# A hybrid decoder layer: the last pair's values in two halves, and the output projection's tiles moved into later steps

## The chip, the cores and the metric

The kernel runs on one core of one Trainium2 chip. The metric is the device time of one execution in microseconds (us). TensorE is called PE below, VectorE DVE, ScalarE ACT, GpSimd POOL; SP issues the transfers.

## The reference

One decoder layer on a sequence of 1024 tokens of width 1024, in float32. The part that matters here is the mixer: eight attention heads of width 64 beside four recurrent heads of width 128, whose outputs are joined and projected.

```python
h = rmsnorm(x, mix_pre_norm[layer])
proj = h @ w_in[layer]
q_a, k_a, v_a, q_h, f_h, i_h, g_h = jnp.split(proj, splits, axis=-1)
attn = dilated_mixture_attention(q_a.reshape(ahead), k_a.reshape(ahead), v_a.reshape(ahead), slopes)
attn = rmsnorm(attn.reshape(B, S, ATTN_WIDTH), attn_out_norm[layer])
rec = hgrn2_recurrence(q_h, f_h, i_h, g_h, lower_bounds[layer], hgrn_out_norm[layer])
mixed = jnp.concatenate([attn, rec], axis=-1) @ w_out[layer]
x = x + rmsnorm(mixed, mix_post_norm[layer])
h = rmsnorm(x, mlp_pre_norm[layer])
ff = jnp.square(jax.nn.relu(h @ w_ff1[layer])) @ w_ff2[layer]
x = x + rmsnorm(ff, mlp_post_norm[layer])
```

## The kernel before

Every float32 product is made of three matmuls in a rounded format: each operand is split into a high part (a copy on ACT, line 83) and a low part (a subtraction on DVE, line 84), and `three_pass` multiplies high by high, high by low and low by high (lines 87 to 89). So each weight tile of 128x1024 costs a transfer (`w_load`), an ACT copy and a DVE subtraction (`w_split`, called through `w_get`), before PE can use it. Two raw tiles are in the chip at a time: a tile's transfer is issued when the tile two places ahead of it in the list has been split.

The recurrent heads come first, then the attention in 64 steps: step s is head s // 8 and block of 128 queries s % 8 (the block number is called b). Heads are taken in pairs (0,1), (2,3), (4,5), (6,7), and a pair shares its projections. A step does in this order: the exponentials of step s+1 (ACT), the scores of step s+2 (`look`: matmuls into one or two banks of tag `s`, read by DVE), the transposes of its own block (`turn`: up to two PSUM banks of tag `t`, emptied by ACT into `pth` and by DVE into `ptl`), the weighted sum of the values (`weigh`, tile `pov`) every other step, the turning back of that sum (`finish`), the step's hook, and then filler. Scores with up to four blocks of keys take one bank, later ones two. At the change of pairs, step 46 for the last pair, the scores of s+2 come only after the transposes, since the next pair's keys must be there.

Filler is PE work from a queue of generators. Each yields an estimated cost of 650 for three matmuls of 128x512, called a unit here, and `fill` takes units until the allowance of the step is used up. `drain` takes all that is left. In heads 0 to 5 the filler is the projection of the next pair (`attn_proj`): its queries (`aq`), values (`av`) and keys (`ak`), each in two halves of 512 tokens with eight units a half. The value halves are turned by four transposes (`v_turn`, tile `pvt`, into a bank of tag `mm`, emptied by ACT and DVE, lines 617 and 618). The second half of the keys is evacuated later (`keys_off`, tile `kf`, through `put_off`), copied into place by ACT, POOL and transfers.

In heads 6 and 7 the filler is `early_out`: the recurrent half of the output projection for the first four row blocks. For a row block t it needs the turned row (`row_turn(t, 0)`: four transposes, tile `pmt`, a bank of tag `t`, split into `emt`) and the first four weight tiles of the output, list places WO0 to WO0+3 (`raw28` to `raw31`). It fills two banks of tag `mm` (`pwe`) at once. The banks of each tag are two, taken in turn. Each engine works through its instructions in the order of the program text; there is no scheduler behind it.

The order around the change is written by hand in `hooks`, by step: before, the output tiles are split in steps 44, 45, 47 and 48, and rows turned in steps 45, 46, 48 and 49. `WO_TAG` says in which buffers the split tiles lie: none means the rotating weight buffers `wh` and `wl`.

Of the kernel before, what the change touches and what calls it, by code (L numbers as in the profile page):

```python
# [18 lines left out]
T = 1024  # L19
# [16 lines left out]
def hymba_layer(ctx, tc, x, w_in, w_out, w_ff1, w_ff2, g_pre, lb_logits, g_mix, g_post,  # L36
# [21 lines left out]
    def half(name, dtype=F32):  # L58
        return sp.tile([P, 512], dtype, tag="half", name=name, bufs=2)
# [63 lines left out]
    def w_get(i, ahead=1):  # L123
        while done[1] < min(i + 1 + ahead, len(stream)):
            w_split()
        return parts[i]
# [24 lines left out]
    for i in range(4 * HH, 4 * HH + 3 * (AH // 2)):  # L151
        stream.append((w_in[i], None))
    WO0 = len(stream)
    WO_TAG = (None, None, ("S", "S"), ("S", "BT"), ("S", "S"), ("S", "T"), ("T", "T"), ("T", "T"))

    def wo_dest(k, tags):
        return lambda: (slab(tags[0], f"woh{k}", F32R), slab(tags[1], f"wol{k}", F32R))
# [25 lines left out]
    def drain():  # L183
        while queue:
            n = len(queue)
            fill(1e9)
            assert len(queue) < n or not queue
# [380 lines left out]
    first_done = [False] * (AH // 2)  # L568
    A0 = 4 * HH

    put_off = []

    def keys_off(pr, stacks, pm, hf):

# [11 lines left out]
    def attn_proj(pr):  # L586
        stacks = [{}, {}]
        box = [None]
        w = w_get(A0 + 3 * pr, 0)
        for i in range(2):  # L590
            stacks[i]["q"] = slab("S", f"q{pr}_{i}", F32R)
        for hf in range(2):
            sl = slice(hf * 512, hf * 512 + 512)
            for n, cost in enumerate(proj_t(w, f"aq{pr}", hf, box)):
                if hf == 0 and n == 4:
                    w_get(A0 + 3 * pr)
                yield cost
            full = half(f"qf{pr}{hf}")
            V.scalar_tensor_tensor(full, box[0], 0.125, rrow[:, sl], op0=ALU.mult, op1=ALU.mult)
            lo = half(f"ql{pr}{hf}", F32R)  # L600
            for i, (a, b) in enumerate(halves):
                S.activation(stacks[i]["q"][a:b, sl], full[a:b], AF.Copy)
                G.tensor_tensor(out=lo[a:b], in0=full[a:b], in1=f32(stacks[i]["q"][a:b, sl]), op=ALU.subtract)
            nc.sync.dma_start(out=f32(stacks[0]["q"][64:128, sl]), in_=f32(lo[0:64]))
            nc.sync.dma_start(out=f32(stacks[1]["q"][0:64, sl]), in_=f32(lo[64:128]))
            yield 650.0
        w = w_get(A0 + 3 * pr + 1, 0)
        vs = slab("V8", f"v{pr}", F32R, (P, NT, 2, 2, 64))
        late = None

        def v_turn(full, hf):
            pt = bank("mm", f"pvt{pr}{hf}")
            for j in range(4):
                TE.transpose(pt[:, j * P:(j + 1) * P], full[:, j * P:(j + 1) * P], ident)
            ptv = pt.rearrange("p (j h d) -> p j h d", j=4, h=2)
            dst = vs[:, hf * 4:hf * 4 + 4]
            S.activation(dst[:, :, :, 0, :], ptv, AF.Copy)
            V.tensor_tensor(out=dst[:, :, :, 1, :], in0=ptv, in1=f32(dst[:, :, :, 0, :]), op=ALU.subtract)
        for hf in range(2):
            sl = slice(hf * 512, hf * 512 + 512)  # L620
            n = 0
            for cost in proj_t(w, f"av{pr}", hf, box):
                n += 1
                if n == 4 and late is not None:
                    v_turn(*late)
                    cost += 450.0
                if n == 5 and hf == 0:
                    w_get(A0 + 3 * pr + 1)
                yield cost
            full = half(f"vf{pr}{hf}")  # L630
            V.tensor_tensor(out=full, in0=box[0], in1=rrow[:, sl], op=ALU.mult)
            late = (full, hf)
            yield 650.0
        while pr > 0 and not first_done[pr - 1]:
            yield None
        w = w_get(A0 + 3 * pr + 2, 0)
        for i in range(2):
            stacks[i]["kh"] = slab("S", f"kh{pr}_{i}", F32R)
            stacks[i]["kl"] = slab("S", f"kl{pr}_{i}", F32R)
        for hf in range(2):  # L640
            sl = slice(hf * 512, hf * 512 + 512)
            n = 0
            for cost in proj_t(w, f"ak{pr}", hf, box):
                n += 1
                if n == 3 and hf == 0:
                    v_turn(*late)
                    cost += 450.0
                if n == 6 and hf == 0:
                    w_get(A0 + 3 * pr + 2)
                yield cost  # L650
            if hf == 0 and pr == AH // 2 - 1:
                early_rows()
            if hf == 0:
                keys_off(pr, stacks, box[0], hf)
            else:
                put_off.append((pr, stacks, box[0], hf))
            pairs[pr] = (stacks, vs)
            yield 650.0
# [6 lines left out]
    def load_bias(hd):  # L665
        if hd < AH and hd not in bts:
            bts[hd] = slab("BT", f"bt{hd}") if hd < AH - 1 else early["table"][:, 0]
            nc.sync.dma_start(out=bts[hd], in_=bias_tab[hd])
# [89 lines left out]
    def load_gain(name, tag, src):  # L758
        gains[name] = slab(tag, name)
        nc.sync.dma_start(out=gains[name], in_=src.partition_broadcast(P))  # L760
# [16 lines left out]
    def early_sums():  # L777
        early["sum"] = [wide.tile([P, 2, D], F32, tag="A", name=f"esum{q}") for q in range(NE // 2)]
# [12 lines left out]
    def row_rec(t):  # L791
        gain = gains["early"] if t < NE else gains["gmix"][:, :AW]
        G.tensor_tensor(out=rec_row(t), in0=rec_row(t), in1=gain, op=ALU.mult)
# [27 lines left out]
    def row_turn(t, which, late=False):  # L821

        if t < NE and which == 0:
            dst = early["mt"][t // 2][:, t % 2]
        else:
            if (t, 1) not in mts and (t, 0) not in mts or t < NE:
                mts[t] = slab("V8", f"mt{t}", F32R, (P, 2, 2, 4, P))
            dst = mts[t][:, which]
        mts[t, which] = dst
        src = rec_row(t) if which == 0 else rows[t][:, AW:]  # L830
        pt = bank("pv" if late else "t", f"pmt{t}_{which}")
        for j in range(4):
            TE.transpose(pt[:, j * P:(j + 1) * P], src[:, j * P:(j + 1) * P], ident)
        split_into(dst[:, 0], dst[:, 1], pt.rearrange("p (j c) -> p j c", j=4))
# [12 lines left out]
    def early_out(t):  # L847
        pms = [bank("mm", f"pwe{t}_{hf}") for hf in range(2)]
        for j in range(4):
            while j >= done[1] - WO0:  # L850
                yield None
            for hf, pm in enumerate(pms):
                sl = slice(hf * 512, hf * 512 + 512)
                three_pass(pm, [mts[t, 0][:, i, j] for i in range(2)], [w[:, sl] for w in parts[WO0 + j]], j == 0, j == 3)
                if j == 3:
                    S.activation(early_sum(t)[:, sl], pm, AF.Copy)
                yield 650.0
# [103 lines left out]
    for h in range(HH):  # L961
# [8 lines left out]

    hooks = {
        43: lambda: [row_rec(0), row_rec(1)],
        44: lambda: [row_rec(2), row_rec(3), w_get(WO0, 0)],
        45: lambda: [drain(), w_get(WO0 + 1, 0), row_turn(0, 0)],
        46: lambda: [early_sums(), row_turn(1, 0), queue.extend(early_out(t) for t in range(NE))],
        47: lambda: [w_get(WO0 + 2, 0), load_bias(AH - 1)],
        48: lambda: [load_gain("gmix", "R", g_mix), w_get(WO0 + 3, 0), row_turn(2, 0)],
        49: lambda: row_turn(3, 0),
        55: lambda: [row_load(t) for t in range(3)],
        59: lambda: [row_norm(0), row_gain(0)],  # L980
        60: lambda: [row_norm(1), row_gain(1)],
# [6 lines left out]
    for s in range(n_steps):  # L988
        if s % 16 == 6:
            first_done[s // 16] = True  # L990
        hd, b = steps[s]
        ready, to_weigh = to_weigh, []
        raise_(s + 1)
        fresh = (s + 2) % 16 == 0
        if not fresh:
            look(s + 2)
        turn(hd, b, exped.pop(s))
        if b % 2:
            to_weigh.append((hd, b // 2))
        to_fold, last_fold = [(i, g, weigh(i, g)) for i, g in ready], to_fold  # L1000
        if fresh and s + 2 < n_steps:
            while pairs[(s + 2) // 16] is None:
                fill(1.0)
            if (s + 2) // 16 + 1 < AH // 2:
                drain()
                queue.append(attn_proj((s + 2) // 16 + 1))
            look(s + 2)
        for i, g, a in last_fold:
            finish(i, g, *a)
        hooks.get(s, lambda: None)()  # L1010
        if b in (7, 0, 1) or s == 46:
            while put_off:
                keys_off(*put_off.pop())
        fill(3240.0 - 340.0 * b if s < n_steps - 20 else 1000.0 if s < n_steps - 16 else 1175.0)
    for i, g, a in to_fold:
        finish(i, g, *a)
    to_fold = [(i, g, weigh(i, g)) for i, g in to_weigh]
# [804 lines left out]
```

## Time and profile before

| | us |
|---|---|
| median of 3 runs | 1268.75 |
| lowest and highest | 1268.53, 1270.63 |
| the profiled execution | 1270.28 |
| its span, first to last instruction | 1268.5 |
| PE busy | 1237.2 |
| DVE busy | 883.2 |
| ACT busy | 532.7 |
| POOL busy | 293.3 |

The mean granted clock of PE over the span is 0.997. The profile gives the busy time of each engine, what ended each idle time of an engine, and a timeline of instructions with their starts. A matmul's row is longer than its share of PE's time, because matmuls are pipelined: the distance between two starts tells what one costs. Rows of DVE and ACT overlap their neighbours by a little for the same reason. The attention steps lie between 310 and 554 us, and step 46 is near 490 us.

### The profile page before, as it was taken

To read this page: it belongs to the slowest core of one execution; us is meant where nothing else is said; L and a number is where in the kernel's file an instruction comes from. 1 tells how busy PE (TensorE), PEld (TensorE's weight loads), DVE (VectorE), ACT (ScalarE), POOL (GpSimd) and SP (SyncE) were. 2 spreads that over 40 slices of the span, in tenths; PEclk is the share of its full clock that TensorE was granted. 3 is DMA by queue.
4 is the path that set the end of the run, shared out by engine and by line. 5 is a ranking of instruction groups with operands and counts; after the bars stand their busy time and mean duration, and the time that the engine had idled before them with its cause. 6 is when DMAs were issued, how large, how long until landed. Compare 5 with 4: busy or idle time off the path is not lost. (4 is left out here: it accounts for less than half of the span.)

```text
span 1268.5 us, 17269 instructions
## 1 busy us (share of the span) xinstructions
PE 1237.2 (98%) x6512; PEld 1056.1 (83%) x6512; DVE 883.2 (70%) x1530; ACT 532.7 (42%) x970; POOL 293.3 (23%) x304
## 2 busy tenths in 40 slices
PE   8999999999999998999999999999999999999997
PEld 8898989888888887877778888888878888888886
DVE  5686868675666666667659766666675777698956
ACT  7523232223565555664565412222236544344412
POOL 0000000012121214044350387557531000000012
PEclk9999999999999999999999999999999999999999
DMA  5201111123232323244342545345368464434413
GB/s 208 68 18 50 34 51 34 34 83 84 68 87 64 88 63 115 96 143 155 100 158 83 207 166 183 126 149 183 125 250 338 155 210 133 156 94 132 168 62 135
DMA packets 58578, 153.98 MB, mean 121 GB/s; under 512 B 4992, under 2 KB 12928, under 8 KB 58240
## 3 DMA queue, kind: packets, MB, share of 16 engines
q1 hardware_dynamic: 58496, 152.89, 35.7%
q8 instruction: 51, 0.84, 0.3%
q14 instruction: 31, 0.25, 0.1%
HBM read 106.73 MB, written 39.85 MB: 116 GB/s over the span
## 5 line engine op out<-in xcount | busy, mean ns | idle before, releaser
L87 PE MATMUL f<-bh,ah 128*128 128x512 f32 x392 | 152.5, 389 | 0.0
L88 PE MATMUL f<-bl,ah 128*128 128x512 f32 x392 | 152.5, 389 | 0.0
L89 PE MATMUL f<-bh,al 128*128 128x512 f32 x392 | 152.5, 389 | 0.0
L84 DVE TENSOR_TENSOR al<-ar,ah 128x1024 fp32r<-128x1024 f32 x49 | 60.6, 1238 | 48.0 <-ACT ah L83 17.6
L88 PEld LDWEIGHTS f<-bl,ah 128*128 128x128 f32 x392 | 73.6, 188 | 15.4
L87 PEld LDWEIGHTS f<-bh,ah 128*128 128x128 f32 x392 | 73.6, 188 | 15.3
L89 PEld LDWEIGHTS f<-bh,al 128*128 128x128 f32 x392 | 73.6, 188 | 15.2
L83 ACT ACTIVATE ah<-ar 128x1024 fp32r<-128x1024 f32 x49 | 52.1, 1064 | 50.1 <-DMA ar<-actd 21.3
L719 DVE TENSOR_TENSOR ptl<-pt,pth 128x512 fp32r<-128x512 f32 (+2 forms) x96 | 50.4, 552 | 23.4 <-ACT pth L718 23.3
L1737 POOL TENSOR_SCALAR fp<-fss 128x1 f32<-128x1 f32 x8 | 3.4, 428 | 266.4 <-ACT fd L1734 266.4
L718 ACT ACTIVATE pth<-pt 128x512 fp32r<-128x512 f32 (+2 forms) x96 | 43.4, 486 | 42.5 <-PE pt L715 41.0
L691 DVE CUSTOM_DVE_ANT_0 p<-ps,bt 128x512 f32<-128x512 f32 (+2 forms) x84 | 44.4, 553 | 19.9 <-PE ps L689 19.7
L1250 POOL TENSOR_TENSOR e<-x,e 128x512 f32<-128x512 f32 x14 | 20.6, 1475 | 136.1 <-DVE x L1201 136.1
L702 ACT ACTIVATE p<-p,nm 128x128 f32<-128x128 f32 (+3 forms) x64 | 49.4, 772 | 2.6 <-DVE nm L695 2.1
L79 POOL TENSOR_SCALAR ms<-hss 128x8 f32<-128x8 f32 x4 | 0.8, 198 | 209.1 <-DVE hss L552 209.1
L715 PE MATMUL pt<-ident,p 128*128 128x128 f32 x288 | 43.0, 276 | 5.4 <-DVE emt L84 3.0
L83 ACT ACTIVATE bh<-br 128x1024 fp32r<-128x1024 f32 x28 | 29.8, 1063 | 43.4 <-PE f L89 38.0
L748 POOL TENSOR_TENSOR anat<-anat,rd 128x128 f32<-128x128 f32 x32 | 14.6, 456 | 129.5 <-DVE anat L747 122.6
L715 PEld LDWEIGHTS pt<-ident,p 128*128 128x128 f32 x288 | 33.6, 141 | 9.9 <-DVE ptl L719 4.0
L732 PE MATMUL pov<-pth,v 128*128 128x256 f32 (+1 forms) x160 | 41.4, 292 | 0.0
L1604 DVE TENSOR_TENSOR acc<-f,acc 128x512 f32<-128x512 f32 x52 | 33.8, 685 | 8.2 <-PE f L89 8.2
L732 PE MATMUL pov<-ptl,v 128*128 128x256 f32 (+1 forms) x160 | 38.6, 286 | 0.5 <-DVE ptl L719 0.5
(1616 smaller groups left out, 3877.5 us busy)
## 6 DMA issues: line engine op xcount, KB each, us to landing
ar<-actd SPq DMA_DIRECT2D x49, 512.0 KB, 3.6
raw<-in_w_in_dram SPq DMA_DIRECT2D x28, 512.0 KB, 3.6
w1r<-in_w_ff_dram SPq DMA_DIRECT2D x14, 1024.0 KB, 6.3
br<-in_w_ff_dram SPq DMA_DIRECT2D x14, 1024.0 KB, 7.8
actd<-e SPq DMA_DIRECT2D x17, 768.0 KB, 4.1
actd<-e SPq DMA_DIRECT2D x11, 1024.0 KB, 4.0
xr<-in_x_dram SPq DMA_DIRECT2D x8, 512.0 KB, 8.6
raw<-in_w_out_dram SPq DMA_DIRECT2D x8, 512.0 KB, 3.5
```

The source lines that it names most:

```text
L83: S.activation(hi, src, AF.Copy)
L84: eng.tensor_tensor(out=lo, in0=src, in1=f32(hi), op=ALU.subtract)
L87: TE.matmul(dst, lhs[0], rhs[0], start=start, stop=False)
L88: TE.matmul(dst, lhs[0], rhs[1], start=False, stop=False)
L89: TE.matmul(dst, lhs[1], rhs[0], start=False, stop=stop)
L691: V.tensor_tensor_reduce(out=pe[:, k0:k0 + n], in0=pS[:, :n], in1=bts[hd][:, o:o + n], scale=1.0, scalar=-3.0e38, op0=ALU.add, op1=ALU.max ...
L702: S.activation(pe[:, :nk], pe[:, :nk], AF.Exp, bias=nm[:, b:b + 1], accum_out=dn[:, b:b + 1])
L715: TE.transpose(pt[:, j * P:(j + 1) * P], pe[:, jj * P:(jj + 1) * P], ident)
L718: S.activation(hi, src, AF.Copy)
L719: V.tensor_tensor(out=lo, in0=src, in1=f32(hi), op=ALU.subtract)
L732: TE.matmul(po[:, c0:256], vst, pt[j // 4][q][:, j % 4, c0:], start=j == 0 and q == 0, stop=j == nj - 1 and q == 1)
L1604: V.tensor_tensor(out=acc_at(p, i), in0=pm, in1=acc_at(p, i), op=ALU.add)
```

## The change

Three things change together, all around the last pair (heads 6 and 7). The number of instructions on PE, DVE and ACT stays the same, and they are of the same shapes.

- The second half of the last pair's values (`av31`) is no longer projected before its keys, in heads 4 and 5, but by a generator of its own, `v_rest`, which is put into the queue in step 45 after the drain. Its turning (`pvt31`) stands in the hook of step 50.
- The first four output tiles are split in steps 48, 49, 50 and 51, the rows turned in steps 48, 51, 52 and 53, and `early_out` joins the queue in step 50. The buffers of the tiles change accordingly: tiles 0 and 1 take slabs, tiles 2 and 3 the rotating buffers.
- The allowance of filler is smaller in steps 30 to 43 (2560 - 270 b, before 3240 - 340 b) and larger from step 48 on (1600, before 1175). The second half of the keys is evacuated in step 47, before in step 46.

In program order PE's filler is afterwards: in step 45 five units (three of the keys, two of `av31`), in step 46 two and in step 47 one of `av31`, in step 48 the turned row 0 and the last three of `av31`, in step 49 none, in step 50 the turning of the values and three units of the output, in steps 51 to 53 a turned row each and two, three and two units, and from step 54 to step 62 two or three units. After the last transposes of step 63 there is none; before there was one.

```diff
-    WO_TAG = (None, None, ("S", "S"), ("S", "BT"), ("S", "S"), ("S", "T"), ("T", "T"), ("T", "T"))
+    WO_TAG = (("S", "S"), ("S", "BT"), None, None, ("S", "S"), ("S", "T"), ("T", "T"), ("T", "T"))
...
+        split = pr == AH // 2 - 1
+
+        def v_rest(wv):
+            sl = slice(512, T)
+            yield from proj_t(wv, f"av{pr}", 1, box)
+            full = half(f"vf{pr}1")
+            V.tensor_tensor(out=full, in0=box[0], in1=rrow[:, sl], op=ALU.mult)
+            yield 650.0
+            rest.append(lambda: v_turn(full, 1))
+        if split:
+            deferred.append(v_rest(w))
-        for hf in range(2):
+        for hf in range(1 if split else 2):
...
-                if n == 6 and hf == 0:
+                if n == 6 and hf == 0 and not split:
                     w_get(A0 + 3 * pr + 2)
...
-        44: lambda: [row_rec(2), row_rec(3), w_get(WO0, 0)],
-        45: lambda: [drain(), w_get(WO0 + 1, 0), row_turn(0, 0)],
-        46: lambda: [early_sums(), row_turn(1, 0), queue.extend(early_out(t) for t in range(NE))],
-        47: lambda: [w_get(WO0 + 2, 0), load_bias(AH - 1)],
-        48: lambda: [load_gain("gmix", "R", g_mix), w_get(WO0 + 3, 0), row_turn(2, 0)],
-        49: lambda: row_turn(3, 0),
+        44: lambda: [row_rec(2), row_rec(3)],
+        45: lambda: [drain(), queue.append(deferred.pop())],
+        46: lambda: load_bias(AH - 1),
+        48: lambda: [w_get(WO0, 0), row_turn(0, 0)],
+        49: lambda: [w_get(WO0 + 1, 0)],
+        50: lambda: [drain(), load_gain("gmix", "R", g_mix), early_sums(), w_get(WO0 + 2, 0), rest.pop()(),
+                     queue.extend(early_out(t) for t in range(NE))],
+        51: lambda: [w_get(WO0 + 3, 0), row_turn(1, 0)],
+        52: lambda: row_turn(2, 0),
+        53: lambda: row_turn(3, 0),
...
-        if b in (7, 0, 1) or s == 46:
+        if b in (7, 0, 1):
...
-        fill(3240.0 - 340.0 * b if s < n_steps - 20 else 1000.0 if s < n_steps - 16 else 1175.0)
+        if s < n_steps - 20:
+            fill(3240.0 - 340.0 * b if s < n_steps - 34 else 2560.0 - 270.0 * b)
+        else:
+            fill(1000.0 if s < n_steps - 16 else 1600.0)
```

More of the change, by code (lines that the diff above doesn't have):

```diff
@@ L569, in hymba_layer @@
     A0 = 4 * HH
-    put_off = []
+    put_off, deferred, rest = [], [], []
     def keys_off(pr, stacks, pm, hf):
```

## The prediction

> **What bounds the kernel now.** I read the busy table of the page first, then who waited for whom on the matmul engine between 310 and 640 us (the attention steps and the output projection behind them), then the stages of 10 us, then the timeline around each idle place; the waits give a total, a count and the longest.
>
> ```profile
> PE 1237.2 (98%) x6512; PEld 1056.1 (83%) x6512; DVE 883.2 (70%) x1530; ACT 532.7 (42%) x970; POOL 293.3 (23%) x304
> ```
>
> ```profile
> 490.00:500.00 10.00, 5.81 (x33) 5.09 (x32) 6.29 (x13) 4.63 (x8) 4.91 (x4) 0.83 0.20 64
> ```
>
> ```profile
> PE pt L715 <- DVE ptl L719: 2.3, 4, 0.9
> ...
> PE pov L732 <- DVE ptl L719: 0.5, 1, 0.5
> ```
>
> PE is busy for 98% of the span, and the change adds or removes no matmul. So the time can move only by what PE idles and by the clock at which it works. The stage from 490 to 500 us is the one sick stage: PE busy 5.81 of 10 us (second figure), granted clock 0.83 (third from the end). It is the change of pairs (steps 45 to 47). The timeline gives the idle times in brackets, each with what ended it:
>
> ```profile
> 466.00 0.33 PE L715 MATMUL pt<-ident,p 128*128 128x128 f32 x1 [0.86 <-DVE ptl L719]
> ...
> 494.07 0.90 PE L715 MATMUL pt<-ident,p 128*128 128x128 f32 x3 [2.98 <-DVE emt L84]
> ...
> 494.99 0.41 PE L732 MATMUL pov<-ptl,v 128*128 128x256 f32 x1
> 495.20 0.41 PE L732 MATMUL pov<-pth,v 128*128 128x256 f32 x1
> ...
> 497.23 0.29 PE L688 MATMUL ps<-kh,q 128*128 128x128 f32 x1
> ...
> 500.11 0.50 PE L87 MATMUL pwe<-wh,emt 128*128 128x512 f32 x1 [1.32 <-DVE kf L577]
> ...
> 504.44 0.28 PE L732 MATMUL pov<-ptl,v 128*128 128x256 f32 x1
> 504.56 0.28 PE L732 MATMUL pov<-pth,v 128*128 128x256 f32 x1
> ...
> 509.54 0.63 PE L833 MATMUL pmt<-ident,erows 128*128 128x128 f32 x4 [1.38 <-DVE emt L84]
> ...
> 523.55 0.75 PEld L715 LDWEIGHTS pt<-ident,p 128*128 128x128 f32 x7 [0.25 <-DVE ptl L719]
> ...
> 547.72 0.63 PE L833 MATMUL pmt<-ident,row 128*128 128x128 f32 x4 [1.26 <-DVE ptl L719]
> ```
>
> The first number of a row is its start, the second its length. The reader is to see that every wait is for VectorE to empty a PSUM bank, and never for data from memory. At 494.07 the transposes of step 46 need a bank of the tag t that the turned row of step 45 (`pmt0_0`) still holds, because its split stands on VectorE behind the split of a weight tile. At 500.11 `pwe0_1` needs the bank from which `kf` is read. After the first gap PE runs slowly: matmuls of 256 columns start 0.21 us apart (494.99 to 495.20), against 0.12 later (504.44 to 504.56).
>
> **What the change removes.** The waits at 494.07 (2.98), 500.11 (1.32) and 509.54 (1.38) lose their cause: no weight tile is split and no row turned in steps 44 to 47, and PE has 15 matmuls of `av31` there. The slow clock between 494.07 and 497.23 goes with the first: 3.16 us x (1 - 0.12/0.21) = 1.35. The wait of 0.86 at 466.00 (start of step 40) goes too: step 39 had no filler, because steps 38 and 39 had used up their allowance, and now has one unit of three matmuls of 512 columns (0.68 us, at the 0.23 each of 511.39 to 511.85 below), and the evacuations of `pvt30` (ScalarE, then VectorE) no longer stand before it. Sum removed: 2.98 + 1.32 + 1.38 + 0.86 + 1.35 = 7.9 us.
>
> Steps 31 to 43 lose eight units of filler. Before ran steps 46 to 60 on one or two units each with a single wait, 0.25 at 523.55, behind the one step that had one unit and two-bank turns (53). Step 37 now is such a step and step 53 no longer, so I count nothing; if the cover fails elsewhere it costs about 0.25 a place. The moved loads cost nothing: `raw28` and `raw29` are in the chip early, the bias of head 7 is wanted at step 54, and `kf` of the second half, one step later, delivers its copies before the wait found below ends.
>
> **What it adds: step 50.** In program order VectorE must do, from step 47 on: `ptl` of block 7, the reduce, `kf31`, the scores of (6,2), `ptl`, the split of tile 0, the row `emt0`, `vf31`, the scores of (6,3), `ptl`, a reduce, the split of tile 1, the scores of (6,4), `ptl`, the split of tile 2, the split of `pvt31`. PE has in the same time four units, and step 49 has none. The durations, all from steps of before with the same instructions:
>
> ```profile
> 499.37 0.68 DVE L577 TENSOR_TENSOR kf<-pm_ak,rrow 128x512 f32<-128x512 f32 x1
> 500.09 1.28 ACT L579 ACTIVATE kh<-kf 64x512 fp32r<-64x512 f32 x2 [1.35 <-DVE kf L577]
> ...
> 501.15 1.04 PE L715 MATMUL pt<-ident,p 128*128 128x128 f32 x8
> ...
> 503.71 0.51 ACT L702 ACTIVATE p<-p,nm 128x256 f32<-128x256 f32 x1
> ...
> 504.01 1.22 DVE L84 TENSOR_TENSOR wol<-raw,woh 128x1024 fp32r<-128x1024 f32 x1
> ...
> 504.28 0.28 ACT L718 ACTIVATE pth<-pt 128x128 fp32r<-128x128 f32 x1
> ...
> 505.14 0.55 DVE L691 CUSTOM_DVE_ANT_0 p<-ps,bt 128x384 f32<-128x384 f32 x1
> ...
> 505.94 0.62 PE L833 MATMUL pmt<-ident,erows 128*128 128x128 f32 x4
> ...
> 506.19 0.38 ACT L735 ACTIVATE ot<-pov 128x256 f32<-128x256 f32 x1 [1.64 <-PE pov L732]
> ...
> 506.48 1.05 ACT L83 ACTIVATE woh<-raw 128x1024 fp32r<-128x1024 f32 x1
> ...
> 507.10 0.39 PE L688 MATMUL ps<-kh,q 128*128 128x512 f32 x1
> ...
> 507.56 1.23 DVE L84 TENSOR_TENSOR wol<-raw,woh 128x1024 fp32r<-128x1024 f32 x1 [1.40 <-ACT woh L83]
> 507.77 0.38 PE L743 MATMUL pov<-ident,ot 128*128 128x128 f32 x2
> ...
> 509.31 0.68 DVE L691 CUSTOM_DVE_ANT_0 p<-ps,bt 128x512 f32<-128x512 f32 x1
> ...
> 510.10 0.41 DVE L719 TENSOR_TENSOR ptl<-pt,pth 128x256 fp32r<-128x256 f32 x1
> ...
> 510.50 0.40 DVE L747 TENSOR_REDUCE anat<-pov 128x128 f32<-128x256 f32 x1
> ...
> 510.83 0.69 DVE L84 TENSOR_TENSOR emt<-pmt,emt 128x512 fp32r<-128x512 f32 x1
> 511.39 0.39 PE L688 MATMUL ps<-kh,q 128*128 128x512 f32 x1
> ...
> 511.85 0.22 PE L688 MATMUL ps<-kh,q 128*128 128x128 f32 x1
> ...
> 512.78 0.45 PE L87 MATMUL pwe<-woh,emt 128*128 128x512 f32 x1
> ```
>
> I count from the start of the eight transposes of step 47 (501.15 in before). `kf31` takes the place that the weight split had there: 504.01 - 501.15 = 2.86. Then 0.72 to the copies `kh` (499.37 to 500.09), and on ScalarE in order 1.28 for them, 0.57 for the exponentials of 256 (503.71 to 504.28), 0.28 for the turned block, 0.29 for `ot` (506.19 to 506.48), and 1.08 from the first half of a weight split to its second on VectorE (506.48 to 507.56). The split of tile 0 starts on VectorE at 7.1. From there VectorE is never idle: 1.13 (504.01 to 505.14), 0.61 each for the row and `vf31` (0.69 less the 0.08 by which rows overlap), 0.61 for the scores of (6,3): 10.1.
>
> PE meanwhile has what it had from 501.15 to 507.91 (the last row, 507.77, and its two transposes at 0.07), which was free of idle time and holds three units; now it is four, so 6.76 + 0.68 = 7.4. Then two matmuls of 512 columns (511.39 to 511.85, 0.46), and at 7.9 the second piece of the scores of (6,4) needs the bank that the scores of (6,3) leave at 10.1. **Wait: 2.2.**
>
> VectorE goes on: 0.18 (rest of the 0.79 of a score row, 509.31 to 510.10), 0.40 for `ptl` and reciprocal (to 510.50), 0.33 for the reduce (to 510.83), 1.13 for tile 1, 1.0 for the scores in two pieces (0.79 and, estimated by its width, 0.2 for a second piece of 128), 0.54 for `ptl` of 384 and reciprocal (estimated between the 0.40 of 256 and the 0.68 that 0.61 for 512 would make), 1.13 for tile 2, 0.61 for `pvt31`: 15.4. PE after its wait: 0.93 (511.85 to 512.78), then 1.16 for four transposes and one unit (505.94 to 507.10), so it stands at 12.2 before `pwe0_1`, whose bank is the one of `pvt31`. **Wait: 3.2.**
>
> **The clock behind it.** 3.2 is longer than the 2.98 that brought the clock down, so I take the same 1.35 again; bounds 0 and twice that.
>
> The Trainium skill ("TensorE: Matmul & The Clock Gate", section "HAM oscillation — how this bites in real kernels") says that idle gaps over about 3.4 us are the ones to avoid. By it neither gap would lower the clock, and the sum would be smaller by the whole term. The trace does not agree: 2.98 was enough, so the row decides.
>
> **What it adds later.** Step 53 turns a row straight after a two-bank turn (block 5); before does this once, at step 61, and waited 1.26 (547.72). Step 52 (block 4) does the same with eight small matmuls between, and its own second bank waits for the row of step 51 behind the split of tile 3. I take 1.1 for both, between 0 and twice 1.26. At the end all the output units are used before the last turn, where before had one unit (0.68) between the last transposes and the `pov` that then still waited 0.5 for them: that wait grows by 0.7. Steps 54 to 60 get more filler and had no idle time to lose.
>
> **The sum.** Added: 2.2 + 3.2 + 1.35 + 1.1 + 1.26 + 0.7 = 9.8. Removed: 7.9. Net **+1.9 us**, on the profiled execution of 1270.28 us (span 1268.5); the median of the runs is 1268.75, so I forecast 1270.6. The bounds (step 52 from -1.1 to +1.4, the VectorE list by 0.5 either way) give 1269.0 to 1272.3. A measurement of this kernel can tell about 0.2%, 2.5 us, from no change.
>
> **Rivals.**
> *The clock holds.* Two gaps with 2 us of work between, instead of one, leave the granted clock at full. Then 1.35 is not paid: +0.5, 1269.3. For it: after the wait of 1.32 the spacing was 0.12 (504.44). Against it: 2.98 was enough. 0.15. This is the case that the skill's rule above would give.
>
> *The tile comes late (slower).* Tile 2 is now fetched only when the split of tile 0 is done and is wanted two steps later.
>
> ```profile
> raw<-in_w_out_dram SPq DMA_DIRECT2D x8, 512.0 KB, 3.5
> ...
> erows<-mixd SPq DMA_DIRECT2D x2, 512.0 KB, 8.5
> ...
> gmix<-in_g_mix_dram SPq DMA_DIRECT2D x1, 512.0 KB, 5.2
> ```
>
> It is issued at 8.2 in the count above, lands 3.5 later at 11.7, and VectorE wants its first half split by 13.6, 1.08 after ScalarE begins: 0.8 to spare. Over 4.3 us of landing it lengthens the second wait one for one: with the 5.2 of `gmix` 0.9 more (1271.5), with the 8.5 of `erows` 4.2 more (1274.8). Nothing else loads then, which speaks against it. 0.12.
>
> *The VectorE list is not late (faster).* If ScalarE reaches the split of tile 0 early enough, the waits of step 50 and their clock do not arise: 1.1 + 1.26 + 0.7 - 7.9 = -4.8, 1263.9. For it: VectorE is busy only 70% of the span. Against it: the list above has no gap from 7.1 on. 0.10.
>
> **Chances.** My forecast 0.63; a third of it lies above 1271.3. Faster 0.10; slower 0.21 + 0.12 = 0.33; within 0.2% 0.42 + 0.15 = 0.57. The range from 1266.8 to 1273.0 leaves out the faster rival and the worst of the late tile.
>
> **What would show it.** Right: no idle time over 1 us on PE between step 44 and step 49; in step 50 two waits, of `ps` for VectorE's score row and of `pwe` for `v` (line 618 of before), near 2.2 and 3.2; a granted clock near 0.83 in the stage of 10 us that follows; waits of `pmt` for `ptl` in steps 52 and 53; the wait at the start of step 40 gone. Wrong: `pwe` waiting for `v` under 1.5 us, or the split of tile 2 waiting for its load, or a new wait between steps 31 and 44.

## The result, and the profile after

| | before, beside it | after |
|---|---|---|
| median, us | 1270.47 | 1274.22 |
| lowest to highest | 1268.53 to 1270.63 | 1273.64 to 1276.28 |
| profiled execution, span | 1270.28, 1268.5 | 1276.28, 1274.5 |
| mean granted clock of the profiled execution | 0.997 | 0.993 |

The ratio is 1.0038 (95% interval 1.0027 to 1.0050): the change makes the kernel slower, and 1274.22 lies above the forecast of 1270.6 and its range (up to 1273.0). The forecast added 1.9 to the 1268.75 of three runs of the kernel before; beside the changed kernel that kernel had a median of 1270.47, so the change cost 3.75 between the medians. The profiled execution of the changed kernel is the slowest of its five.

Ratios below are always to the kernel before on the same chip; 0.0010 is 1.27 us. A ratio is not the quotient of the two medians, which here is 1.0030. The variants ran on three chips, on which the kernel before had medians of 1269.67 (the first four experiments), 1270.14 and 1270.43, so a median of a variant is set against the 1274.22 with care.

The busy table of the changed kernel, the line of PE, and then who waited for whom on PE from 430 to 645 us (total, count, longest):

```profile
PE 1243.0 (98%) x6512; PEld 1059.9 (83%) x6512; DVE 884.2 (69%) x1530; ACT 532.2 (42%) x970; POOL 292.4 (23%) x304
```

```profile
PE pwe L87 <- DVE v L618: 3.0, 1, 3.0
PE pmt L844 <- DVE ptl L730: 2.9, 3, 1.1
...
PE ps L699 <- DVE mx L702: 1.9, 1, 1.9
PE pov L743 <- ACT pth L729: 1.2, 1, 1.2
```

The same instructions, and 5.8 us more of busy time: PE was slower at its work, which busy time includes. The two waits of step 50 are there, of `pwe` for `v` and of `ps` for the score row. The stages of 10 us of the changed kernel show the clock (third figure from the end; the first after the length is PE's busy time):

```profile
490.00:500.00 10.00, 8.14 (x55) 7.05 (x53) 7.14 (x20) 6.77 (x15) 2.97 (x3) 1.00 0.37 94
500.00:510.00 10.00, 7.00 (x35) 5.74 (x34) 6.17 (x17) 4.47 (x10) 1.25 (x1) 0.83 0.67 223
510.00:520.00 10.00, 8.04 (x47) 6.51 (x45) 7.47 (x21) 6.77 (x14) 1.31 (x1) 1.00 0.24 76
550.00:560.00 10.00, 8.46 (x56) 7.40 (x55) 7.07 (x13) 8.56 (x17) 4.20 (x7) 0.96 0.31 98
560.00:570.00 10.00, 9.47 (x38) 7.91 (x37) 3.39 (x5) 3.45 (x9) 1.24 (x3) 0.70 0.74 265
590.00:600.00 10.00, 7.63 (x30) 6.14 (x31) 7.90 (x11) 4.92 (x15) 3.46 (x10) 0.83 0.34 123
```

At half clock for x us, a stage of 10 us shows 1 - x / 20. A window inside such a stretch, in which PE is busy throughout, shows that the clock is halved there (0.50):

```profile
505.50:507.50 2.00, 2.00 (x6) 1.54 (x6) 0.00 (x0) 0.00 (x0) 0.00 (x0) 0.50 1.00 313
```

So there are 3.4 us at half clock after 500, 6.8 around 560 and 3.4 after 590, where before had one such stretch, after 490. Beside these only the end of the kernel, where PE has no work left, is below full clock, in both. The timeline of PE in the changed kernel shows where they begin:

```profile
499.29 0.33 PE L699 MATMUL ps<-kh,q 128*128 128x128 f32 x1 [1.86 <-DVE mx L702]
...
504.66 0.80 PE L87 MATMUL pwe<-woh,emt 128*128 128x512 f32 x1 [3.00 <-DVE v L618]
505.25 0.63 PE L88 MATMUL pwe<-wol,emt 128*128 128x512 f32 x1
505.68 0.63 PE L89 MATMUL pwe<-woh,emt 128*128 128x512 f32 x1
...
509.40 0.48 PE L87 MATMUL pwe<-woh,emt 128*128 128x512 f32 x1
509.71 0.40 PE L88 MATMUL pwe<-wol,emt 128*128 128x512 f32 x1
509.95 0.40 PE L89 MATMUL pwe<-woh,emt 128*128 128x512 f32 x1
...
512.53 0.33 PE L726 MATMUL pt<-ident,p 128*128 128x128 f32 x1 [0.24 <-DVE emt L84]
...
514.46 0.66 PE L844 MATMUL pmt<-ident,erows 128*128 128x128 f32 x4 [0.71 <-DVE ptl L730]
...
520.13 0.66 PE L844 MATMUL pmt<-ident,erows 128*128 128x128 f32 x4 [1.13 <-DVE ptl L730]
...
557.69 0.39 PE L743 MATMUL pov<-pth,v 128*128 128x256 f32 x1 [1.20 <-ACT pth L729]
558.42 0.39 PE L743 MATMUL pov<-ptl,v 128*128 128x256 f32 x1 [0.34 <-DVE ptl L730]
...
562.95 0.77 PE L87 MATMUL pwo<-woh,mt 128*128 128x512 f32 x1
...
581.84 1.03 PE L936 MATMUL ph<-ident,esum 128*128 128x128 f32 x8
...
591.57 1.06 PE L936 MATMUL ph<-ident,esum 128*128 128x128 f32 x8 [1.93 <-DVE esum L926]
593.43 0.79 PE L87 MATMUL pwo<-woh,mt 128*128 128x512 f32 x1 [0.80 <-ACT mt L83]
```

What VectorE did before the second wait of step 50: the splits of tiles 0, 1 and 2, then the subtraction for `v`, in the order of the list in the prediction:

```profile
496.20 1.23 DVE L84 TENSOR_TENSOR wol<-raw,woh 128x1024 fp32r<-128x1024 f32 x1 [0.86 <-ACT woh L83]
...
500.06 1.22 DVE L84 TENSOR_TENSOR wol<-raw,woh 128x1024 fp32r<-128x1024 f32 x1
...
502.80 1.21 DVE L84 TENSOR_TENSOR wl<-raw,wh 128x1024 fp32r<-128x1024 f32 x1
503.92 0.68 DVE L618 TENSOR_TENSOR v<-pvt,v 128x512 fp32r<-128x512 f32 x1
```

Matmuls of 512 columns start 0.43 us apart behind the wait at 504.66 (505.25 to 505.68) and 0.24 apart later (509.71 to 509.95). Two landmarks of the kernel before, first matmul of `pwo` and first of `ph`, from its timeline:

```profile
559.18 0.48 PE L87 MATMUL pwo<-woh,mt 128*128 128x512 f32 x1
...
576.61 1.03 PE L925 MATMUL ph<-ident,esum 128*128 128x128 f32 x8
```

The changed kernel is 3.77 behind at the first (562.95 less 559.18) and 5.23 at the second: 1.46 more in a stretch in which PE waits for nothing in either kernel. It is the slow stretch around 560, and no list of waits has it.

### The profile page after: what moved, and what is told of

Read it like the earlier page. It is cut to its first block, busy times and chain, and to the rows that moved or that the text cites. A ratio compares the mean times of both kernels' runs of the same rounds, so it can differ in the third digit from the quotient of the medians.

```text
span 1274.5 us, 17261 instructions
## 1 busy us (share of the span) xinstructions
PE 1243.0 (98%) x6512; PEld 1059.9 (83%) x6512; DVE 884.2 (69%) x1530; ACT 532.2 (42%) x970; POOL 292.4 (23%) x304
## 5 line engine op out<-in xcount | busy, mean ns | idle before, releaser
L1268 POOL TENSOR_TENSOR e<-x,e 128x512 f32<-128x512 f32 x14 | 20.7, 1475 | 137.1 <-DVE x L1219 137.1
```

## The experiments

Several add unread matmuls: 128x512 products into a bank that nobody reads, put into a place where PE waits. They are meant to shorten no wait of the rest; PE is only busy while it waits. The helper for them is

```python
def spin(tag, n, rhs):
    d = bank(tag, f"spin{tag}")
    lhs = pairs[3][1][:, 0, 0].rearrange("p a d -> p (a d)")
    for _ in range(n):
        TE.matmul(d, lhs, rhs, start=True, stop=True)
```

**Fill the longest wait of step 50.** In `early_out`:

```diff
+                if t == 0 and j == 0 and hf == 1:
+                    spin("pv", 12, pairs[3][0][0]["q"][:, :512])
```

> The changed kernel with 12 matmuls of 128x512 whose result nobody reads, put into PE's order right before pwe0_1 of step 50, into a free bank. They fill 12 x 0.227 = 2.7 us of the 3.0 us wait; no wait of VectorE gets shorter and no real work moves. Clock theory (the waits of the two kernels are equal, 13.0 against 13.4 us from 430 to 645 us; what the change costs is PE at half clock for whole windows of about 3.4 us behind each window in which it idled for more than about half): the window after step 50 stays at full clock, about 1.7 us less than the changed kernel, near 1272.5. Wait theory (the time is the waits of steps 50, 53 and the end): no difference, near 1274.2.

Measured: 1272.83 (1272.09 to 1276.71), ratio 1.0028 (1.0019 to 1.0037). The profiled execution took 1272.36 with a clock of 0.998; its other waits up to 590 us are those of the changed kernel, and the one at `pwo` near 617 is 1.49, where the changed kernel has 0.19. The median is 1.4 lower than 1274.22, but that of the kernel before is 0.8 lower on this chip too. By the ratio 1.3 us came back without a wait becoming shorter, as the clock theory has it; the intervals of the two ratios overlap, so by itself this is weak.

**Fill the wait at the end too.** Beside the edit above, after the last `finish` of step 63:

```diff
+    spin("s", 5, early["mt"][1][:, 0, 0].rearrange("p j c -> p (j c)"))
```

> As e1_spin50, and 5 more such matmuls between the last transposes of step 63 and the pov that waits there (1.2 us). Clock theory: the two slow windows from 559 to 566 us go as well, 3 us more: near 1269.5 to 1271, with slow windows left only where another wait of 1.9 us (near 590 us) falls into one window. Wait theory: near 1274.2, or 0.2 more.

Measured: 1272.77 (1271.72 to 1273.96), ratio 1.0021 (1.0012 to 1.0030). The gain that I expected, to 1269.5 to 1271, did not come. The stages of the profiled execution, the slowest of this kernel, suggest why:

```profile
500.00:510.00 10.00, 10.00 (x50) 8.59 (x49) 6.66 (x19) 4.91 (x10) 1.25 (x1) 0.83 0.71 229
550.00:560.00 10.00, 9.61 (x64) 8.23 (x62) 7.07 (x12) 8.56 (x17) 4.48 (x7) 1.00 0.33 102
560.00:570.00 10.00, 9.47 (x49) 7.86 (x47) 3.87 (x6) 4.17 (x11) 3.74 (x10) 1.00 0.83 292
590.00:600.00 10.00, 9.68 (x35) 7.79 (x36) 7.90 (x11) 4.92 (x15) 3.79 (x10) 0.69 0.33 111
```

The end is clean now (1.00 twice), but slow stretches began behind the first wait of step 50, still open, and behind the wait of `ph`. Filling only some of the places is no test, since a slow stretch can begin behind another.

**Rows into one-bank steps.** `row_turn(2, 0)` moved from hook 52 to 50, `row_turn(3, 0)` from 53 to 56.

> The changed kernel with the rows 2 and 3 turned in steps 50 and 56 instead of 52 and 53, that is only in steps whose own turn takes one bank. Both theories: the waits of pmt for ptl (0.71 and 1.13 us) go, and 0.4 us of the wait before pwe0_1 is filled by the transposes of row 2: 2.2 us less, near 1272. Clock theory adds that the slow windows stay (behind step 50, at the end), so no more than that; wait theory the same. It prices the term of steps 52 and 53 by itself.

Measured: 1271.18 (1270.16 to 1273.99), ratio 1.0015 (1.0006 to 1.0024). The waits of 0.71 and 1.13 are gone as expected and the `pwe` wait fell to 2.6; the median is 3.0 lower than 1274.22, where I had expected 2.2. Against the kernel before on the same chip it lies 1.5 above instead of 3.75, which is 2.2 less. The slow stretches stayed in the profiled execution, as expected (0.83 in the stages after 500 and 590, 0.84 and 0.82 from 550 to 570).

**One unit kept for the end.** The allowance of steps 56 to 63 is 1475 instead of 1600.

> The changed kernel with an allowance of 1475 instead of 1600 in steps 56 to 63, so that one unit of the output (0.68 us) is left between the last transposes of step 63 and the pov that waits for them, as in the kernel before. Wait theory: 0.7 us less, near 1273.5. Clock theory: the wait there falls from 1.2 + 0.34 to about 0.5, the window before 559 us idles less than half, and the two slow windows behind it go: 0.7 + 2 to 3 us less, near 1271.

Measured: 1272.79 (1271.51 to 1273.72), ratio 1.0021 (1.0012 to 1.0029). The 1.20 and 0.34 at the end became one wait of 0.51, as before, 1.0 less. The median is 1.4 lower than 1274.22, between the two theories; against the kernel before on the same chip only 0.6 of that is left, so it decides nothing. In the profiled execution the stages from 550 to 570 us were at full clock (1.00 and 1.00), those from 500 and from 590 were not (0.83 each): the place that was mended stayed clean, the others did not.

**Values before the tile.** In hook 50 `rest.pop()()` stands ahead of `w_get(WO0 + 2, 0)`.

> The changed kernel with one pair of calls exchanged in the hook of step 50: the values are turned before tile 2 is split. VectorE's subtraction for v then stands in front of that tile's 1.13 us, and pwe0_1 is freed so much earlier. VectorE-list theory (step 50 waits for a list of splits that VectorE works through without a gap): the wait falls from 3.0 to about 1.9, and the time by 1.1, a little more where the shorter wait also spares a slow window: 1272 to 1273. If the wait were set by something else (the load of tile 2, ScalarE), it would stay near 3.0 and the time at 1274.2.

Measured: 1275.06 (1271.94 to 1275.42), ratio 1.0036 (1.0024 to 1.0049). The wait did exactly what was expected, in the profiled execution:

```profile
503.88 0.50 PE L87 MATMUL pwe<-woh,emt 128*128 128x512 f32 x1 [1.87 <-DVE v L618]
```

3.00 became 1.87, and the median did not fall. A part of the gain was lost again soon after: the wait for `emt` in step 52 (510.65) is 0.68, where the changed kernel has 0.24. The execution with 1271.94, the one with a trace, had a clock of 0.996; three at 1275.06 to 1275.42 had 0.991. So a wait can shrink by 1.1 us and the time not fall, and what sets the slow executions apart is their clock. There are only five, and no trace of a slow one. Still, this was the plainest sign that the list of waits is not the account.

**The same on the kernel before.** 11 unread matmuls in the wait of 2.98, ahead of the transposes of step 46.

> The kernel before with 11 unread matmuls (2.5 us) inside its 2.98 us wait at the change of pairs (between the two banks of transposes of step 46). No wait gets shorter. If a window that idles for more than about half costs the next one its clock, the slow window from 494 to 497 us goes and the median falls by up to 1.35, the lowest times (which by their clock of 0.999 had no slow window) stay at 1268.4: near 1268.7. If the clock does not matter, 1269.7.

Measured: 1269.42 (1268.50 to 1270.48), ratio 0.9998 (0.9989 to 1.0007). Inconclusive: the median lies between the two values, and the interval includes 1. The wait of `ph` was left open here, as in the second experiment.

**The kernel before once more**, unchanged, with a profile.

> The kernel before once more, for a second trace. The waits of PE stay where they are to 0.1 us; whether and where it shows slow windows is another draw of the window's phase: a second trace without one after the 2.98 us wait would show that the phase decides, one with it that the wait alone does.

Measured: 1270.47, clock 0.996. The waits did not stay where they were: ahead of the transposes of step 46 stands 1.82 now, and 0.52 for POOL's `erows` ahead of the turned row before them, where the first trace had 2.98 in one. The slow stretch behind them is there again:

```profile
490.00:500.00 10.00, 6.40 (x35) 5.26 (x33) 6.27 (x14) 4.74 (x8) 5.99 (x5) 0.83 0.22 69
```

So at this place the two traces agree. The stage from 580 to 590 us, first of the profiled execution of before, then of this one:

```profile
580.00:590.00 10.00, 7.28 (x39) 5.47 (x38) 7.22 (x11) 5.59 (x16) 3.94 (x10) 1.00 0.44 151
```

```profile
580.00:590.00 10.00, 7.96 (x37) 6.22 (x36) 7.23 (x11) 5.59 (x16) 4.02 (x10) 0.83 0.42 151
```

The same instructions with the same wait of 1.92 for `ph`: once the clock holds, once it is halved for 3.4 us. A wait of this size is not always followed by a slow stretch. That the moment at which it falls decides is my guess; no run shows it.

**All the places filled, in both kernels.** In the changed one 7 and 12 in the two waits of step 50, 5 at the end, and 7 ahead of the first `ph`; in the one before 10 in step 46 and 7 ahead of the first `ph`.

```diff
+            if (hd, b, pc) == (6, 4, 1):
+                spin("pv", 7, pairs[3][0][0]["q"][:, :512])
...
+            if t == 0 and kh == 0:
+                m = mts[2, 1]
+                for _ in range(7):
+                    TE.matmul(pt, m[:, 0, 0], m[:, 0].rearrange("p j c -> p (j c)"), start=True, stop=True)
```

> The changed kernel with all four places filled behind which a slow stretch began: unread matmuls of 128x512 stand in both waits of step 50 (7 and 12), in the wait at the end of step 63 (5) and in the wait for the first ph (7); the waits themselves keep their length. Theory (what exceeds the forecast is slow clock): granted clock 0.998 or more in nearly every run, no stretch at half clock, median 1271 to 1271.8, and 2 above the kernel before with its own two places filled, which is what the waits alone add up to. Rival (a lasting cost beside clock and waits): the clock rises too, but the median stays at 1272.3 or more, 3.2 above the kernel before so filled.

> The kernel before with unread matmuls in the wait of step 46 (10) and in the wait for the first ph (7). Theory (slow clock is a part of its time too, and of its scatter of 3 us): clock 0.998 or more in nearly every run, median 1269.0, scatter under 1 us. Rival: the median of the kernel before, 1270, and the same scatter.

Measured: the changed kernel so filled 1272.02 (1271.45 to 1272.79), ratio 1.0014 (1.0005 to 1.0022); the one before 1269.38 (1267.94 to 1270.30), ratio 0.9991 (0.9982 to 1.0000). Every execution of both had a clock of 0.998 or 0.999. The seven ahead of `ph` stood 10 us too early, at the first `ph`, which waits for nothing; they delayed PE by 1.6 and shortened the wait at the second from 1.93 to 0.74, so nothing moved behind it. No stage of either but the last is below 1.00. Stages of the changed kernel, filled:

```profile
500.00:510.00 10.00, 9.70 (x55) 8.11 (x55) 7.70 (x22) 5.87 (x12) 1.61 (x2) 1.00 0.71 241
...
550.00:560.00 10.00, 9.08 (x62) 7.74 (x61) 7.04 (x11) 8.19 (x18) 4.55 (x6) 1.00 0.36 106
560.00:570.00 10.00, 10.00 (x51) 8.35 (x50) 3.78 (x6) 4.38 (x11) 3.63 (x9) 1.00 0.88 316
590.00:600.00 10.00, 10.00 (x49) 8.32 (x49) 7.24 (x11) 5.12 (x16) 3.44 (x9) 1.00 0.31 107
```

and its timeline in step 50:

```profile
501.83 2.88 PE L865 MATMUL spinpv<-q,v 128*128 128x512 f32 x12
505.01 0.50 PE L87 MATMUL pwe<-woh,emt 128*128 128x512 f32 x1 [0.30 <-DVE v L618]
```

The product of the unit starts no earlier, 505.01 against 504.66, and the clock is full. Freed of slow clock, the changed kernel lies 2.64 above the one before so freed, between the 2 of the clock theory and the 3.2 of its rival. The clock costs the changed kernel 2.2 of its median (1274.22 to 1272.02; the intervals of the two ratios do not overlap) and the one before 1.05 (1270.43, its median on that chip, to 1269.38). So the clock is a part of the cost of the change, and by these medians not the larger one. The medians of 1272.02 and 1269.38 are above what I expected (1271 to 1271.8, and 1269.0). The scatter of the kernel before, which I expected under 1 us, is still 2.4 in eleven executions at a clock of 0.998 to 0.999; unfilled it was 3.0 in thirty-three. Here the clock is not the whole of it.

**The tiles and the values in other steps.** Tile 0 is split in step 45, 1 in 48, 2 in 50, 3 in 51, the values are turned in step 49, the keys evacuated in step 46; rows and allowances as in the changed kernel.

```diff
-        45: lambda: [drain(), queue.append(deferred.pop())],
+        45: lambda: [drain(), w_get(WO0, 0), queue.append(deferred.pop())],
...
-        48: lambda: [w_get(WO0, 0), row_turn(0, 0)],
-        49: lambda: [w_get(WO0 + 1, 0)],
-        50: lambda: [drain(), load_gain("gmix", "R", g_mix), early_sums(), w_get(WO0 + 2, 0), rest.pop()(),
-                     queue.extend(early_out(t) for t in range(NE))],
+        48: lambda: [w_get(WO0 + 1, 0), row_turn(0, 0)],
+        49: lambda: [drain(), load_gain("gmix", "R", g_mix), early_sums(), rest.pop()()],
+        50: lambda: [w_get(WO0 + 2, 0), queue.extend(early_out(t) for t in range(NE))],
...
-        if b in (7, 0, 1):
+        if b in (7, 0, 1) or s == 46:
```

> The changed kernel with the tiles split in steps 45, 48, 50 and 51 and the values turned in step 49, the keys evacuated in step 46; rows and allowances as in the changed kernel. Theory (both waits of step 50 go, 4.9, and the slow clock behind them, 1.5; the rows' waits of 0.7 and 1.1 and the end's stay): 1267.5 to 1268.7. Rival (the clock's windows take back most of what a wait gives, as when the values were turned earlier): 1270 to 1272.

Measured: 1268.18 (1267.55 to 1271.08), ratio 0.9985 (0.9977 to 0.9994). This is what I expected. Both waits of step 50 are gone. The times fall into two groups: 1267.55 to 1268.23 at a clock of 0.997 to 0.999, and 1270.85 to 1271.08 at 0.994. The groups lie 3 us apart, and the clock is all that is known to tell them apart; there is no trace of a slow one.

**The same with the rows and the end mended.** Rows turned in steps 48, 50, 56 and 57, and the allowance 1475 in the last eight steps.

> The changed kernel with the deferred values kept and the rest spread: tile 0 split in step 45 (VectorE idles there), tile 1 in 48, tile 2 in 50, tile 3 in 51; the values turned in step 49; the second half of the keys evacuated in step 46 again; rows turned in steps 48, 50, 56 and 57, all with one-bank turns; one unit kept for the end. VectorE-list theory: the waits of step 50 (1.86 and 3.0) shrink to under 1.5 together, those of pmt (0.71, 1.13) go, the end loses 0.7, and with fewer long waits fewer slow windows: 6 to 8 us less than the changed kernel, 1266 to 1268, below the kernel before. If deferring the values costs something by itself, it stays above 1269.7.

Measured: 1264.28 (1263.94 to 1264.72), ratio 0.9957 (0.9944 to 0.9969): faster than both kernels, and than I expected. PE's waits from 430 to 645 us in it:

```profile
PE ph L936 <- DVE esum L926: 1.9, 1, 1.9
PE pmt L844 <- DVE ptl L730: 1.1, 1, 1.1
...
PE pvt L614 <- DVE vf L625: 0.6, 1, 0.6
```

**That version without the deferral.** The second half of the values is projected early again (`split = False`), with the tile buffers and the allowance of steps 30 to 43 as in the kernel before.

> The variant that is faster than both kernels (tiles split in steps 45, 48, 50, 51, rows turned in 48, 50, 56, 57), with the second half of the last pair's values projected early again, as before: only the deferral is undone. Theory (the deferral is what pays, since steps 46 to 49 have no other filler): 1268 to 1270, with idle time of 1 us a step on the matmul engine from step 46 to 49. Rival (the places of the tiles pay): 1264 to 1265.5.

Measured: 1269.07 (1268.68 to 1271.57), ratio 0.9994 (0.9985 to 1.0003). It is as fast as the kernel before: spreading the tiles alone gains nothing that can be measured. Its timeline has three waits that the version with the deferral has not, at the starts of steps 40 and 48 and in step 50, and not one in each step as expected:

```profile
466.21 0.33 PE L726 MATMUL pt<-ident,p 128*128 128x128 f32 x1 [0.86 <-DVE ptl L730]
...
497.26 0.47 PE L726 MATMUL pt<-ident,p 128*128 128x128 f32 x1 [2.48 <-DVE ptl L730]
...
504.77 0.33 PE L699 MATMUL ps<-kh,q 128*128 128x128 f32 x1 [2.11 <-DVE mx L702]
```

So the deferral pays 4.8 us (1269.07 less 1264.28, on two chips; 4.7 by the ratios), if the tiles' work on DVE is spread; as the change placed it, the kernel lost 3.75.

## Why the prediction was wrong

The measured median lies 3.6 above the forecast, and this falls into three parts. 1.7 is the base: the forecast was built on 1268.75, the median of three runs, and beside the changed kernel it was 1270.47, though the profiled execution of 1270.28 was known too. This part is chance, and no step of the argument. 1.1 is slow clock: the change costs 3.75, and 2.64 with the waits filled in both kernels. The last 0.7 (2.64 against the 1.9 that the waits were to add) stays open. The step that failed is the price of the clock.

**What is removed: right.** There is no idle time over 1 us from step 44 to step 49, and the 0.86 at step 40 is gone. The size of the largest term is not a constant: the 2.98 stood behind a weight split of 2.31 on DVE, which took 1.88, 1.54 and 2.15 in three other executions of that code, beside products on POOL that lay differently (in the second trace of before it was two waits, 0.52 and 1.82).

**Step 50: right.** 2.2 and 3.2 were forecast, 1.86 and 3.00 came, in the places named. The rival that the list would not be late fell, and so did the late tile: the second wait is not longer than forecast, and it is for `v`. The slow stretch came too, in the stage named (0.83).

**Steps 52, 53 and the end: nearly right.** 1.1 forecast, 0.24 + 0.71 measured; 1.26 forecast, 1.13 measured; the end 0.7 forecast, 1.20 + 0.34 less the 0.51 of before, 1.03, measured.

Without the clock my terms were 8.5 added and 6.5 removed. Added were 1.86 + 3.00 + 0.95 + 1.13 + 1.03 = 8.0. What is left of the difference is the wait of 1.26 at 547.72, now 1.07. All the idle times that the timelines bracket from 300 us to the first `pwo` are 12.36 after and 11.12 before.

**The clock behind it: wrong.** I put one slow stretch of 1.35 behind step 50 against the one of 1.35 removed, so the clock weighed nothing in the net; the bounds of nothing and twice that, which I gave for it, did not enter the bounds of the sum (whose own terms reach 1272.5, not 1272.3). The waits at the end of the attention and before `ph` had no slow stretch in the sum at all. From the filled changed kernel the prices in the profiled execution can be read as distances between the same matmuls: 504.66 to 509.40 is 4.74 against 3.20 filled, so 1.54 behind step 50; 558.42 to 562.95 is 4.53 against 3.15, so 1.38; the first `pwo` to the first `ph` (in the filled kernel, to the first unread matmul ahead of it) 18.89 against 17.42, so 1.47; together 4.4. The stretch behind 593 costs nothing, since a wait of 1.5 at the `pwo` near 616 in the kernel before shrinks to 0.19. In the same way the one stretch of before cost 1.5. The net is 2.9 in the pair of profiled executions, where I had zero; 1.1 between the medians, since the profiled execution is the slowest of five.

The account of the profiled pair: idle 1.24, clock 1.4 to the first `pwo` and 1.5 from there to the first `ph`, start 0.25 (the transposes at 364.00 us stand at 364.26 after, but also in the second trace of before, so this is no effect of the change), which makes 4.4 of the 6.0. The rest, 0.85 before the first `pwo` and 0.8 behind the first `ph`, lies in no idle time that the view brackets, and stays open (0.6 of the 0.8 arise between 661 and 704 us, at the start of the feed-forward part, which the change leaves alone); the filled pair, too, differs by more than the idle times, 2.64 against 1.24.

What was wrong in the argument was to price the clock by the wait that I had added, as if the 2.98 were a threshold. I had two more places, 0.51 and then 0.53 at the end of the attention, to which I added 0.7, and the 1.92 for `ph`, and asked of neither what the clock would do behind it. The rival of a clock that holds was on the wrong side. The Trainium skill ("TensorE: Matmul & The Clock Gate", section "A second HAM failure mode: psum-queue depth-cycling") says that frequent short idle places between groups of matmuls, as banks are passed on, were enough in another kernel to make the clock swing; this case agrees in that slow stretches came behind waits of 1.20 + 0.34 (559 us) and of 1.93 + 0.80 (593 us).

What stays open beside that: how much idle time within which stretch brings the clock down. Behind each of the five unfilled waits of 2.48 to 3.00 the traces have a slow stretch (before, the changed kernel, the rows, the one unit, and the version without the deferral). Shorter waits are mixed: the 1.9 before `ph` has one behind it in eight of twelve traces, the 1.20 + 0.34 at the end in two of five.

## What to carry to other kernels

When an engine's clock follows its activity, a wait costs its length plus, in some executions, a slow stretch behind it: list every idle place of 1 us or more that the change leaves, old ones too, and put a price on each in the range. To tell the two costs apart, fill the waits, all of them and in both kernels, with unread matmuls, and compare the filled pair. And before moving work on the evacuating engine, count it step by step: the same tile splits and the same turning of the values, up to three steps earlier, with the keys one step earlier, moved the ratio from 1.0038 to 0.9985.

## What the runs showed of the hardware

- A stretch at half clock is about 3.4 us or twice that (stages at 0.83, and at 0.96 and 0.70 together), whatever the wait before it was. Each 3.4 us cost 1.4 to 1.5 us, or nothing where a later wait took it up (the one after 590).
- The clock is a part of the scatter of a kernel. With the waits filled the changed kernel scatters by 1.3 us at a clock of 0.998 to 0.999, unfilled by 2.6 at 0.991 to 0.997; the kernel before scatters by 2.4 filled, at 0.998 to 0.999, and by 3.0 unfilled, at 0.994 to 0.999.
- The same DVE subtraction of 128x1024 took 1.23 alone and 1.54 to 2.31 beside POOL's products for `erows` (2.31 and 1.88 in two executions of the kernel before); with it the wait behind it moved. POOL lost too: its four products took 5.97 there and 5.05 in the version with rows and end mended, where no such subtraction stands beside them. Where the subtraction began first (504.01, in the prediction), it stayed at 1.22, and POOL's product for `anat`, 0.40 with no subtraction beside it (510.99), took 1.25. The rows of DVE and POOL at the change of pairs, first of the profiled execution of before, then of the kernel before with 11 unread matmuls:

```profile
491.11 2.31 DVE L84 TENSOR_TENSOR wl<-raw,wh 128x1024 fp32r<-128x1024 f32 x1 [0.64 <-ACT wh L83]
...
488.57 5.97 POOL L793 TENSOR_TENSOR erows<-erows,etable 128x512 f32<-128x512 f32 x4 [3.72 <-DMA erows<-mixd]
```

```profile
491.78 1.54 DVE L84 TENSOR_TENSOR wl<-raw,wh 128x1024 fp32r<-128x1024 f32 x1 [0.64 <-ACT wh L83]
...
490.95 3.52 POOL L795 TENSOR_TENSOR erows<-erows,etable 128x512 f32<-128x512 f32 x2 [0.83 <-DMA erows<-mixd]
```
